# A decoder trunk on one core: the first product of every weight chunk in two halves of 128 columns

## The chip, the core and the metric

The kernel runs on one core of a Trainium2 chip. Its engines work at the same time, each on its own queue: TensorE (PE; its weight loads are listed as PEld), VectorE (DVE), ScalarE (ACT), GpSimd (POOL) and SyncE (SP), which issues most transfers here. The metric is the device time of one execution in microseconds.

## The reference

Two decoder layers over 256 tokens of width 2048, in float32. Cut to what matters:

```python
for l in range(DEPTH):                                   # DEPTH = 2
    u = rms_norm(h, norm1_g[l])
    (sc_x, sc_c, sc_b, m_cq, m_ckv, m_kr, g_q, g_k, g_v, g_z, g_a, g_b,
     r_q, r_f, r_i, r_z) = split_cols(u @ w_in[l])       # w_in: 2048 x 5840
    y_sc  = ...    # gated short convolution
    y_mla = ...    # latent attention: low-rank q, k, v by w_uq, w_ukv
    y_gdn = ...    # gated delta rule, chunks of 64
    y_hg  = ...    # HGRN2 recurrence, chunks of 64
    h = h + jnp.concatenate([y_sc, y_mla, y_gdn, y_hg], axis=-1) @ w_o[l]
    v_ff = rms_norm(h, norm2_g[l])
    h = h + jnp.square(jax.nn.relu(v_ff @ w_ff1[l])) @ w_ff2[l]   # 2048 -> 8192 -> 2048
return rms_norm(h, final_g)
```

## The kernel before

All weights pass once through the core as streams, one for each group of output columns: gk, krab, gz, gq, rz, gv, rf, rq, ri, cq, ckv, uqn, uqr, uk, uv, sx, sc, sb (the mixer), wo0 to wo3, and the MLP in four quarters q, each with four streams f1_q_0 to f1_q_3 (FF1) and four f2_q_0 to f2_q_3 (FF2). A stream has kt tiles of 128 rows (16 of them for a contraction over 2048) and m columns, mostly 512.

`stream` works through its weights in chunks. `_chunks` makes a chunk as many k-tiles as divide kt and fit 2048 columns: 4 k-tiles at m = 512 or 384, 8 at 256, all 16 at 72 (krab), and the whole stream for uqn (3 k-tiles, m = 512), uqr (3, 256) and uk (2, 512). `fetch` (L323) brings a chunk into one of three raw buffers over SP's queue. In pieces of up to 1024 columns ScalarE rounds it to fp32r, Ht (L354), and VectorE subtracts to get the rest, Lt (L355); there are four buffers of each. The activations (u, u2) are kept as such a pair too, `a[:, 0]` and `a[:, 1]`, 256 tokens wide. A product of the reference is then three matmuls: high x high, high x low, low x high.

In most streams the weights are the stationary operand and the 256 tokens pass through: for each column group j of 128 columns, for each k-tile of the chunk, L404, L405 and L406, adding up in one half of a PSUM bank. These are the 256-column streams. uv, wo and FF2 are token-major: the activations are stationary and 512 columns of weights pass (L368 to L370), in another branch of `stream`. The first product of a bank clears it (`start=`). For the six names in `HALVES` the very first product of the stream, and only that one, is issued as two matmuls of 128 tokens (L402) with the same weights:

```python
begin, end = opens and first and i == 0, closes and final and i == kc - 1
if begin and j == 0 and key in HALVES:
    for t in (slice(0, P), slice(P, T)):
        PE.matmul(o[:, t], lhsT=Hk[:, ms], rhs=a[:, 0, t], start=t.start == 0, stop=False)
else:
    PE.matmul(o, lhsT=Hk[:, ms], rhs=a[:, 0, :], start=begin, stop=False)
PE.matmul(o, lhsT=Hk[:, ms], rhs=a[:, 1, :], start=False, stop=False)
PE.matmul(o, lhsT=Lk[:, ms], rhs=a[:, 0, :], start=False, stop=end)
```

The mixer's own small matmuls (L711 to L1155; L971 is the HGRN2 levels, L873 and L877 the delta rule's steps) stand between the streams' products on TensorE. The order of each engine's instructions is set by a planner that plays the program through with estimated times; rounding, subtraction, transfers and evacuations have been given a high priority.

Of the kernel before, what the change touches and what calls it, by code (L numbers as in the profile page):

```python
# [33 lines left out]

COL = dict(sx=0, sc=512, sb=1024, cq=1536, ckv=1920, kr=2176, gq=2240, gk=2752, gv=3264, gz=3776,
           ab=4288, rq=4296, rf=4808, ri=5320, rz=5832)


HALVES = ("rz", "rf", "rq", "f1_1_0", "f1_2_0", "f1_3_0")

# [1 line left out]
def _chunks(kt, m):  # L44

    kc = max(c for c in range(1, kt + 1) if kt % c == 0 and c * m <= RAW_ELEMS)
    kp = min(kc, max(1, PIECE_ELEMS // m))
    if kp > 2:
        while kc % kp:
            kp -= 1  # L50
    return kc, kp
# [146 lines left out]
class Slots:  # L198
# [6 lines left out]
    def get(self, shape, dtype=F32):  # L205
        assert self.free, "no slot left"
        i = self.free.pop(0)
        self.low = min(self.low, len(self.free))
        self.k += 1
        t = self.pool.tile([shape[0], SLOT], dtype, tag=f"slot{i}", name=f"sl{self.k}", bufs=1)  # L210
        n = int(np.prod(shape[1:]))
        assert n <= SLOT
        v = t[:, :n]
        if len(shape) == 3:
            v = v.rearrange("p (a b) -> p a b", a=shape[1])
        elif len(shape) == 4:
            v = v.rearrange("p (a b c) -> p a b c", a=shape[1], b=shape[2])
        self.of[id(v)] = (i, v)
        return v
# [8 lines left out]
def trunk(ctx: ExitStack, tc: tile.TileContext, xT, x_d, fg_d, pos, wpk, par_d, cst_d, msk_d, out):  # L228
    nc = tc.nc
    V, S, G, PE = nc.vector, nc.scalar, nc.gpsimd, nc.tensor  # L230
# [75 lines left out]
    def main_bank(name):  # L306
        return psx.tile([P, 512], F32, tag="m", name=name, bufs=NMAIN)


    def fetch(l, key, c, between=None):  # L310
        off, kt, m = info[l, key]
        kc, _ = _chunks(kt, m)
        n = kc * m
        o = off + c * P * n
        raw = wp.tile([P, RAW_ELEMS], F32, tag="raw", name="raw", bufs=3)
        with tc.high_priority(AHEAD):
            src = wpk[l][o : o + P * n].rearrange("(p n) -> p n", p=P)

            for i in range(2 if between else 1):
                z = slice(i * n // 2, (i + 1) * n // 2) if between else slice(0, n)  # L320
                if between:
                    between(c * kc + i * kc // 2, c * kc + (i + 1) * kc // 2)
                nc.sync.dma_start(raw[:, z], src[:, z])  # L323
        return raw

    def stream(l, key, rhs, evac=None, order=None, token_major=None, banks=None, start=0, wide=False):

        off, kt, m = info[l, key]
        kc, kp = _chunks(kt, m)
        nm = (m + P - 1) // P
        if banks is not None:
            pss = banks
        elif token_major is None:
            pss = [main_bank(f"ps_{key}") for j in range(0, nm, 1 if wide else 2)]
        else:  # L340
            pss = [main_bank(f"ps_{key}") for j in range(2)]
        order = order or range(kt // kc)
        seen = start
        for c in order:
            early = l == 0 and key == "gk"
            raw = fetch(l, key, c, load_x if early else None)
            parts = []
            for k0 in range(0, kc, kp):
                ke = min(kp, kc - k0)
                src = raw[:, k0 * m : (k0 + ke) * m]  # L350
                Ht = wp.tile([P, PIECE_ELEMS], F32R, tag="H", name="Ht", bufs=4)
                Lt = wp.tile([P, PIECE_ELEMS], F32R, tag="L", name="Lt", bufs=4)
                with tc.high_priority(AHEAD):
                    S.copy(Ht[:, : ke * m], src)  # L354
                    V.tensor_tensor(Lt[:, : ke * m], src, Ht[:, : ke * m].bitcast(F32), ALU.subtract)  # L355
                H3 = Ht[:, : ke * m].rearrange("p (k m) -> p k m", k=ke)
                L3 = Lt[:, : ke * m].rearrange("p (k m) -> p k m", k=ke)
                parts += [(H3[:, k], L3[:, k], rhs(c * kc + k0 + k)) for k in range(ke)]
            first, final = seen == 0, seen + kc == kt
            seen += kc  # L360
            if early:
                first_split(c * kc, c * kc + kc)
            if token_major:
                for j in range(2):
                    ps, ms = pss[j], slice(j * P, j * P + P)
                    for i, (Hk, Lk, a) in enumerate(parts):
                        begin, end = first and i == 0, final and i == kc - 1
                        PE.matmul(ps, lhsT=a[:, 0, ms], rhs=Hk, start=begin, stop=False)  # L368
                        PE.matmul(ps, lhsT=a[:, 1, ms], rhs=Hk, start=False, stop=False)  # L369
                        PE.matmul(ps, lhsT=a[:, 0, ms], rhs=Lk, start=False, stop=end)  # L370
                    if final:
                        with tc.high_priority(AHEAD):
                            evac(j, ps)
                continue
            for j in range(nm if wide else 0):
                ps, ms = pss[j], slice(j * P, j * P + P)
                for i, (Hk, Lk, a) in enumerate(parts):
                    begin, end = first and i == 0, final and i == kc - 1

                    def high():  # L380
                        PE.matmul(ps, lhsT=Hk[:, ms], rhs=a.rearrange("p a t -> p (a t)"), start=begin, stop=end)

                    def low():
                        PE.matmul(ps[:, T:], lhsT=Lk[:, ms], rhs=a[:, 0, :], start=False, stop=False)

                    for f in (low, high) if end else (high, low):
                        f()
                if final:
                    with tc.high_priority(AHEAD):
                        evac(j, ps)  # L390
            for j in range(0 if wide else nm):
                ps = pss[j // 2]
                w = min(P, m - j * P)
                ms = slice(j * P, j * P + w)
                o = ps[:w, j % 2 * T : j % 2 * T + T]
                opens, closes = j % 2 == 0, j % 2 == 1 or j == nm - 1
                for i, (Hk, Lk, a) in enumerate(parts):
                    begin, end = opens and first and i == 0, closes and final and i == kc - 1
                    if begin and j == 0 and key in HALVES:

                        for t in (slice(0, P), slice(P, T)):
                            PE.matmul(o[:, t], lhsT=Hk[:, ms], rhs=a[:, 0, t], start=t.start == 0, stop=False)  # L402
                    else:
                        PE.matmul(o, lhsT=Hk[:, ms], rhs=a[:, 0, :], start=begin, stop=False)  # L404
                    PE.matmul(o, lhsT=Hk[:, ms], rhs=a[:, 1, :], start=False, stop=False)  # L405
                    PE.matmul(o, lhsT=Lk[:, ms], rhs=a[:, 0, :], start=False, stop=end)  # L406
                if final and closes:
                    n = j % 2 + 1
                    with tc.high_priority(AHEAD):
                        evac(j // 2, ps[:w, : n * T].rearrange("p (a t) -> p a t", a=n), n)  # L410
        return pss
# [120 lines left out]
    def first_split(k0, k1):  # L532

        with tc.high_priority(AHEAD):
            for k in range(k0, k1):
                scaled_split(u, k, xs[k // 4][:, k % 4], pc(0, "n1", k))
# [85 lines left out]
    for l in range(DEPTH):  # L622
# [41 lines left out]

        rawk = get((P, NH, T))
        stream(l, "gk", ua, to_slot(rawk))
        stream(l, "krab", ua, ev_krab)
        nc.scalar.dma_start(kr[64:, 0], kr[:64, 0])
        swap32(kr[:, 1], kr[:, 0])
# [3 lines left out]

        gz = get((P, NH, T))
        stream(l, "gz", ua, to_slot(gz))

        na = tmp.tile([8, 1], F32, tag="na", name="na", bufs=1)
# [8 lines left out]
        for tb in range(2):  # L686
            for i, src in enumerate((la, sg)):
                o = (tb * 2 + i) * 8
# [73 lines left out]
        rz = get((P, NH, T))  # L762
# [351 lines left out]
        for tb in range(2):  # L1114
# [5 lines left out]
            for g in range(NH // per):  # L1120
                ps = xps((P, per, n), "sc")
                for i in range(per):
# [3 lines left out]
                              start=False, stop=True)  # L1126
# [86 lines left out]
        for q in range(4):  # L1213
            a8 = [get((P, 2, 2, T), F32R) for _ in range(8)]
            a = lambda k, a8=a8: a8[k // 2][:, k % 2]
# [80 lines left out]
```

## Time and profile before

| | us |
|---|---|
| median of 3 runs | 2332.02 (2331.19 to 2332.23) |
| the profiled execution | 2331.44 |
| its span | 2329.7 |
| TensorE busy | 2296.3 |
| VectorE busy | 1416.7 |
| ScalarE busy | 1126.0 |
| GpSimd busy | 252.7 |

The span runs from the first to the last instruction of one profiled execution. An engine's busy time counts an instant once, however many of its instructions overlap there. Layer 0 lies at 0 to 1168 us (mixer up to 467, then the MLP), layer 1 behind it (mixer up to 1618).

### The profile page before, as it was taken

What the parts mean: (1) busy time and instruction counts of PE and PEld (TensorE: products, weight loads), DVE (VectorE), ACT (ScalarE), POOL (GpSimd) and SP (SyncE); (2) the same over time, 40 slices, a digit from 0 to 9 for tenths busy, and PEclk for the clock granted to TensorE, in tenths of its full rate; (3) what the DMA queues carried; (4) which work ended last, traced back from release to release, by engine and by line L of the source; (5) the groups of instructions that cost most, each with busy time, mean ns of one, the idle gap of its engine ahead of it and who ended that gap; (6) DMA issues with size and microseconds to landing.
All of it is one profiled execution on the core that took longest, in us unless ns stands there. A gap on an engine that the chain in (4) does not pass through costs nothing.

```text
span 2329.7 us, 38035 instructions
## 1 busy us (share of the span) xinstructions
PE 2296.3 (99%) x16060; PEld 2131.0 (91%) x16060; DVE 1416.7 (61%) x1585; ACT 1126.0 (48%) x1392; POOL 252.7 (11%) x175
## 2 busy tenths in 40 slices
PE   8999999999999999999999999999999999999997
PEld 8999999899899899899899998988988988988986
DVE  8888686555545545555578867865554554555454
ACT  6554555554344344344455647555443443443443
POOL 2322210000000000000013114000100100100100
PEclk9999999999999999999999999999999999999999
DMA  7453245555555555555545532555555555556553
GB/s 287 165 184 130 90 168 181 183 195 189 194 198 191 192 197 193 190 195 196 184 164 176 181 130 99 170 184 175 195 197 197 186 198 197 188 195 215 191 193 122
DMA packets 63754, 422.46 MB, mean 181 GB/s; under 512 B 7136, under 2 KB 10080, under 8 KB 15200
## 3 DMA queue, kind: packets, MB, share of 16 engines
q1 hardware_dynamic: 62656, 419.13, 51.7%
q8 instruction: 125, 2.05, 0.3%
q10 hardware_dynamic: 928, 0.92, 0.2%
q14 instruction: 45, 0.37, 0.0%
HBM read 417.00 MB, written 2.10 MB: 180 GB/s over the span
## 4 chain that ended last, share of the span: by engine, by line
PE 95%; DVE 3%; ACT 1%; issue 1%; DMA 0%; POOL 0%; SPq 0%; ACTq 0%; DVEq 0%
PE ps_f L405 10%; PE ps_f L406 10%; PE ps_f L370 10%; PE ps_f L369 10%; PE ps_f L368 10%; PE ps_f L404 10%; PE ps_wo L369 3%; PE ps_wo L368 2%; PE ps_wo L370 2%; PE lv L971 1%; DVE Lt L355 1%; PE ps_gq L404 1%; PE ps_gq L406 1%; PE ps_sb L404 1%; PE ps_gq L405 1%; PE ps_sb L406 1%
## 5 line engine op out<-in xcount | busy, mean ns | idle before, releaser
L355 DVE TENSOR_TENSOR Lt<-raw,Ht 128x1024 fp32r<-128x1024 f32 (+2 forms) x790 | 983.4, 1263 | 758.3 <-ACT Ht L354 736.3
L354 ACT CAST Ht<-raw 128x1024 fp32r<-128x1024 f32 (+2 forms) x790 | 804.5, 1043 | 852.9 <-PE ps_f L369 346.8
L405 PE MATMUL ps_f<-u,Ht 128*128 128x256 f32 x2048 | 565.9, 276 | 0.0
L406 PE MATMUL ps_f<-u,Lt 128*128 128x256 f32 x2048 | 565.5, 276 | 0.0
L404 PE MATMUL ps_f<-u,Ht 128*128 128x256 f32 x2042 | 563.7, 276 | 0.0
L370 PE MATMUL ps_f<-Lt,sl 128*128 128x512 f32 x1024 | 399.0, 390 | 0.0
L369 PE MATMUL ps_f<-Ht,sl 128*128 128x512 f32 x1024 | 398.5, 389 | 0.0
L368 PE MATMUL ps_f<-Ht,sl 128*128 128x512 f32 x1024 | 398.4, 389 | 0.0
L405 PEld LDWEIGHTS ps_f<-u,Ht 128*128 128x128 f32 x2048 | 384.5, 188 | 0.1
L406 PEld LDWEIGHTS ps_f<-u,Lt 128*128 128x128 f32 x2048 | 384.4, 188 | 0.0
L404 PEld LDWEIGHTS ps_f<-u,Ht 128*128 128x128 f32 x2042 | 383.3, 188 | 0.1
L369 PEld LDWEIGHTS ps_f<-Ht,sl 128*128 128x128 f32 x1024 | 192.2, 188 | 39.8
L370 PEld LDWEIGHTS ps_f<-Lt,sl 128*128 128x128 f32 x1024 | 192.2, 188 | 39.7
L368 PEld LDWEIGHTS ps_f<-Ht,sl 128*128 128x128 f32 x1024 | 192.2, 188 | 39.5
L1224 POOL TENSOR_TENSOR sl<-sl,sl 128x512 fp32r<-128x512 f32 x64 | 83.1, 1299 | 1316.1 <-ACT sl L1223 1105.3
L368 PE MATMUL ps_wo<-Ht,sl 128*128 128x512 f32 x256 | 100.5, 392 | 0.0
L370 PE MATMUL ps_wo<-Lt,sl 128*128 128x512 f32 x256 | 100.3, 393 | 0.0
L369 PE MATMUL ps_wo<-Ht,sl 128*128 128x512 f32 x256 | 99.8, 390 | 0.0
L1223 ACT CAST sl<-sl 128x512 fp32r<-128x512 f32 x64 | 39.8, 622 | 81.6 <-DVE sl L1222 81.6
L521 DVE SCALAR_TENSOR_TENSOR h<-ps_f,r2sq,h 128x512 f32<-128x512 f32 x64 | 47.9, 748 | 26.1 <-PE ps_f L370 26.1
L1221 ACT ACTIVATE sl<-ps_f 128x512 f32<-128x512 f32 x64 | 38.0, 593 | 49.4 <-PE ps_f L406 49.4
L1222 DVE TENSOR_TENSOR sl<-ps_f,sl 128x512 f32<-128x512 f32 x64 | 43.8, 685 | 23.4 <-ACT sl L1221 23.4
(404 smaller groups left out, 3636.5 us busy)
## 6 DMA issues: line engine op xcount, KB each, us to landing
raw<-w SPq DMA_DIRECT2D x376, 1024.0 KB, 4.8
raw<-w SPq DMA_DIRECT2D x10, 768.0 KB, 4.3
raw<-w SPq DMA_DIRECT2D x12, 512.0 KB, 7.5
sl<-xT SPq DMA_DIRECT2D x8, 256.0 KB, 7.8
h<-x SPq DMA_DIRECT2D x2, 1024.0 KB, 10.7
y<-h SPq DMA_DIRECT2D x8, 256.0 KB, 4.0
raw<-w SPq DMA_DIRECT2D x2, 576.0 KB, 7.2
sl<-fg SPq DMA_DIRECT2D x2, 512.0 KB, 4.7
```

Source lines behind the costliest of these rows:

```text
L354: S.copy(Ht[:, : ke * m], src)
L355: V.tensor_tensor(Lt[:, : ke * m], src, Ht[:, : ke * m].bitcast(F32), ALU.subtract)
L368: PE.matmul(ps, lhsT=a[:, 0, ms], rhs=Hk, start=begin, stop=False)
L369: PE.matmul(ps, lhsT=a[:, 1, ms], rhs=Hk, start=False, stop=False)
L370: PE.matmul(ps, lhsT=a[:, 0, ms], rhs=Lk, start=False, stop=end)
L404: PE.matmul(o, lhsT=Hk[:, ms], rhs=a[:, 0, :], start=begin, stop=False)
L405: PE.matmul(o, lhsT=Hk[:, ms], rhs=a[:, 1, :], start=False, stop=False)
L406: PE.matmul(o, lhsT=Lk[:, ms], rhs=a[:, 0, :], start=False, stop=end)
L521: V.scalar_tensor_tensor(z, ps, scale[:, tb : tb + 1], z, ALU.mult, ALU.add)
L1222: V.tensor_tensor(s_, ps, b_, ALU.mult)
L1223: S.copy(a2[:, :, 0, :], s_)
L1224: G.tensor_tensor(a2[:, :, 1, :], s_, a2[:, :, 0, :].bitcast(F32), ALU.subtract)
```

## The change

`HALVES` goes. Every chunk of a 256-column stream now issues its first product (column group 0, first k-tile) as two matmuls of 128 tokens each, with the same weights. Only where that product also opens the stream does its first half clear the bank; in later chunks both halves add to what is there.

```diff
-HALVES = ("rz", "rf", "rq", "f1_1_0", "f1_2_0", "f1_3_0")
...
                     begin, end = opens and first and i == 0, closes and final and i == kc - 1
-                    if begin and j == 0 and key in HALVES:
+                    if i == 0 and j == 0:
 
                         for t in (slice(0, P), slice(P, T)):
-                            PE.matmul(o[:, t], lhsT=Hk[:, ms], rhs=a[:, 0, t], start=t.start == 0, stop=False)
+                            PE.matmul(o[:, t], lhsT=Hk[:, ms], rhs=a[:, 0, t], start=begin and t.start == 0, stop=False)
                     else:
                         PE.matmul(o, lhsT=Hk[:, ms], rhs=a[:, 0, :], start=begin, stop=False)
```

## Rows read from the trace of the kernel before

**Rows 1.** The page: busy time by engine, and the last chain by engine.

```profile
PE 2296.3 (99%) x16060; PEld 2131.0 (91%) x16060; DVE 1416.7 (61%) x1585; ACT 1126.0 (48%) x1392; POOL 252.7 (11%) x175
...
PE 95%; DVE 3%; ACT 1%; issue 1%; DMA 0%; POOL 0%; SPq 0%; ACTq 0%; DVEq 0%
```

**Rows 2.** The page's groups: count, busy us and mean ns, idle before.

```profile
L404 PE MATMUL ps_f<-u,Ht 128*128 128x256 f32 x2042 | 563.7, 276 | 0.0
```

**Rows 3.** Busy time by stretch: length, engines in order, granted clock, DMA share, GB/s.

```profile
0.00:46.10 46.10, 38.40 (x272) 36.38 (x273) 37.44 (x57) 28.37 (x48) 11.75 (x17) 0.96 0.80 293
...
171.30:209.50 38.20, 36.82 (x323) 36.42 (x321) 35.79 (x57) 21.35 (x24) 10.84 (x3) 1.00 0.40 148
...
267.30:300.80 33.50, 28.46 (x200) 25.53 (x199) 24.32 (x29) 27.82 (x43) 14.70 (x8) 1.00 0.26 87
...
467.50:1168.20 700.70, 700.70 (x4644) 640.29 (x4644) 361.31 (x343) 311.86 (x354) 41.56 (x32) 1.00 0.55 193
...
1332.90:1342.40 9.50, 8.91 (x80) 8.71 (x78) 9.50 (x14) 6.86 (x9) 3.69 (x2) 1.00 0.31 110
...
1418.00:1451.40 33.40, 28.36 (x199) 25.46 (x198) 24.25 (x29) 27.72 (x42) 14.67 (x8) 1.00 0.25 86
```

**Rows 4.** Timeline where f1_1_0 opens: start us, us, engine, line, instruction.

```profile
642.68 0.33 PE L402 MATMUL ps_f<-u,Ht 128*128 128x128 f32 x2
642.79 0.19 PEld L405 LDWEIGHTS ps_f<-u,Ht 128*128 128x128 f32 x1
642.85 0.33 PE L405 MATMUL ps_f<-u,Ht 128*128 128x256 f32 x1
642.90 0.19 PEld L406 LDWEIGHTS ps_f<-u,Lt 128*128 128x128 f32 x1
643.02 0.28 PE L406 MATMUL ps_f<-u,Lt 128*128 128x256 f32 x1
643.02 0.19 PEld L404 LDWEIGHTS ps_f<-u,Ht 128*128 128x128 f32 x1
643.14 0.28 PE L404 MATMUL ps_f<-u,Ht 128*128 128x256 f32 x1
```

**Rows 5.** Line 402: duration ns min/median/max, first and last start us.

```profile
L402 PE MATMUL ps_f<-u,Ht x12: 222/248/273, 642.7 to 2141.8; 128*128 128x128 f32 x12
```

**Rows 6.** Timeline of TensorE at f1_1_0's second chunk, and where FF2 begins.

```profile
648.13 0.28 PE L406 MATMUL ps_f<-u,Lt 128*128 128x256 f32 x1
648.24 0.28 PE L404 MATMUL ps_f<-u,Ht 128*128 128x256 f32 x1
...
729.84 0.39 PE L368 MATMUL ps_f<-Ht,sl 128*128 128x512 f32 x1
```

**Rows 7.** Timeline of TensorE where rq opens.

```profile
166.31 0.33 PE L402 MATMUL ps_rq<-u,Ht 128*128 128x128 f32 x2
166.48 0.33 PE L405 MATMUL ps_rq<-u,Ht 128*128 128x256 f32 x1
166.65 0.28 PE L406 MATMUL ps_rq<-u,Lt 128*128 128x256 f32 x1
```

**Rows 8.** TensorE's waits: who waited for whom, total us, times, longest.

```profile
PE it L1065 <- ACT sl L1066: 3.6, 2, 1.8
PE ps_uv L370 <- DVE Lt L355: 3.3, 2, 1.7
PE ps_gk L406 <- DVE Lt L355: 2.6, 3, 1.6
PE ps_krab L406 <- DVE Lt L355: 1.9, 1, 1.9
PE ps_gk L404 <- ACT Ht L354: 1.3, 2, 0.8
...
PE ps_ri L406 <- DVE Lt L355: 0.6, 1, 0.6
```

**Rows 9.** TensorE alone by stretch, the same columns; the granted clock follows the count.

```profile
40.70:44.00 3.30, 3.30 (x18) 0.50 0.88 290
```

## The prediction

> **What bounds the kernel now.** I read the page's busy shares and its chain first: TensorE is busy for 2296.3 us of a span of 2329.7 us, and 95% of the chain that ended last is its own work [rows 1]. A matmul's busy time overlaps its neighbour's (a 256-column product is drawn 276 ns long [rows 2]), so that share alone does not say that TensorE is full; the starts in the timelines do [rows 4, 6]. In the second of the four quarters of layer 0's MLP the FF1 streams open at 642.68 us, with two halves that are there already, and the first FF2 product starts at 729.84 us [rows 4, 6]. Between them the code issues 4 streams x 16 k-tiles x 4 column groups x 3 = 768 products, one of them in two halves: 769 matmuls in 87.16 us, **0.1133 us each**, one slot. Sixteen chunks of weights begin in that time. I looked at one: the second chunk begins 4 x 4 x 3 + 1 = 49 slots after 642.68, at 648.24 us, and it starts 0.11 after the product ahead of it, like every other one [rows 6]. So there is no bubble at a chunk's beginning that two shorter products could fill. In that MLP VectorE is busy for 361 of 700.7 us and ScalarE for 312 [rows 3]; the chunks are ready in time.
>
> TensorE does wait in two places. At the start of layer 0 it is fed too slowly: 38.4 us busy of the first 46.1 [rows 3], with waits of 2.6, 1.9 and 1.3 us for Lt and Ht in gk and krab [rows 8]. In the middle of each layer, around the attention groups, it waits for the other engines: 1.38 us of 171.3 to 209.5, 5.04 of 267.3 to 300.8, and in layer 1 0.59 of 1332.9 to 1342.4 and 5.04 of 1418.0 to 1451.4 [rows 3]. That is 12.05 us in all.
>
> **The change, counted.** Until now only the very first product of six named streams was halved. Now the first k-tile of column group 0 of every chunk is. By the chunk rule (as many k-tiles as fit 2048 columns, dividing the k count) a layer's mixer has 11 streams of 512 columns with 4 chunks each (44), cq 4, ckv 2, krab 1, and uqn, uqr and uk 1 each: 54. FF1 has 16 streams of 4: 64. That is 118 a layer, 236 in all, 12 of them halved already, so **224 matmuls and 224 weight loads are added**, 122 in FF1 and 102 in the mixer. The wo, uv and FF2 streams take another branch. Nothing is removed, and no transfer, copy or subtraction is added. Both halves need what the whole product needed (the same Ht, the same tile of u), so nothing can start earlier.
>
> **Its price.** The trace holds the very operation, 24 halves of it. At 642.68 the pair starts; the next product (L405) starts at 642.85, the one behind it (L406) at 643.02, and from there on the starts are 0.11 to 0.12 apart again [rows 4]. From the first half to L406 it is 0.34 us, where two whole products take 2 x 0.1133 = 0.227. So a halved product costs 0.113 us more, a whole slot, although it streams the same 256 columns. The columns themselves do pass in half the time: the pair is drawn 0.33 us long and a half lasts up to 273 ns, so the second starts some 0.06 after the first [rows 4, 5]. But the weight loads behind the pair start at 642.79, 642.90 and 643.02, not closer than 0.11 [rows 4], and every matmul here brings its own. I read it so: loads have a pace of 0.11 us, like a 256-column product, and an extra load pushes all behind it by one slot. In rq, where 256-column products and not 512-column ones stand ahead of the pair, it is 166.31 to 166.65, 0.34 again [rows 7]. No row shows a pair at a chunk in mid-stream; rq's is the nearest, and I see no difference in kind. I take 0.1133. The starts are given to 0.01 us, and two readings agree, so I let it be 0.108 to 0.118.
>
> **What of it lies on the path.** The 122 in FF1 all do, since TensorE never pauses there: 122 x 0.1133 = 13.8 us. Of the 102 in the mixer:
> - The four of gk and the one of krab in layer 0 stand among waits for Lt and Ht of up to 1.9 us [rows 8], released by VectorE and ScalarE, which the pairs do not delay. These five cost nothing; with that cover gone, 0.6 us.
> - uqn, uqr and uk of both layers (six) come ahead of uv's two waits, 3.3 us together, for Lt, which VectorE writes [rows 8]: nothing, or 0.7 us uncovered.
> - VectorE is busy for 35.8 of the 38.2 us from 171.3 in layer 0 and for all 9.5 us from 1332.9 in layer 1, and there TensorE ends up waiting [rows 3] (0.6 us for ri's Lt in layer 1 [rows 8]). Eight chunks begin there (rq's second to fourth and ri's first three in layer 0, rq's fourth and ri's first in layer 1). But VectorE's own pieces wait for Ht, whose buffers TensorE gives back. So I let half of the eight be hidden, 4, with 0 and 8 as ends.
>
> That leaves 224 - 5 - 6 - 4 = 209 on the path, 209 x 0.1133 = **23.7 us**. Nothing else becomes late behind it: what follows a chunk's products (evacuations, the next pieces) moves with them, and the weight transfers gain 0.11 us per chunk.
>
> **Two side effects, bounded.** The clock: from 40.7 to 44.0 us the granted clock is 0.50, so 1.2 GHz [rows 9], after TensorE has stood for 1.9 us ahead of krab's first Lt [rows 8]. Eighteen matmuls pass in 3.3 us instead of 29: 11 x 0.1133 = 1.25 us lost. The pairs shorten the standstill by some 0.1 us only, so I let this stay as it is; it may go (-1.25) or come a second time (+1.25). The order: the small products of the mixer are placed between the streams by a planner that follows estimated times, and 224 more matmuls change its input. The two layers have different orders already, as the stalls show: 1.38 us against 0.59 in the stretches where ri begins [rows 3]. That is 0.8 us a layer, 1.6 in both, either way.
>
> **Sum.** The profiled execution took 2331.44 us (the span of 2329.7 and 1.7 around it), 0.58 under the runs' median of 2332.02. 2331.44 + 23.7 = 2355.1; on the median's scale 2355.7 us, 1.0% longer. Low end: 224 - 5 - 6 - 8 = 205 on the path at 0.108 are 22.1, less 1.25 and 1.6: 19.3, on the median 2351.3. High end: all 224 at 0.118 are 26.4, with 1.25, 1.6 and one more stall like the longest of the mixer (1.8 [rows 8]) 31.1: 2363.1.
>
> **Rivals.**
> 1. *The second load is hidden (not slower).* The place is the pair: the second half's load, the same weights again, runs beside the first half, and L405's beside the second. Then a pair takes twice the 0.06 between its halves, 0.12, and costs 0.007 us more than a whole product: 209 x 0.007 = 1.5 us, 2333.5 us, no change. It decides from the point at which L405 starts 0.12 behind the first half; the rows show 0.17, and another 0.17 to L406 [rows 4, 7]. Against it stands every pair of the trace. 3%. The Trainium skill's page "TensorE: Matmul & The Clock Gate", section "Back-to-back issue gap", would have it this way: it gives 134 cycles for 128 columns and 262 for 256, by which (an estimate from that page) a pair costs 2.5 ns and all 224 cost 0.6 us. The trace does not agree for this stream.
> 2. *Half hidden.* At a chunk in mid-stream only the 0.17 us to L405 is paid and L406 keeps its slot: a pair costs 0.057 us, 209 x 0.057 = 11.9, 2343.9 us. For it speaks only that the trace has no pair in mid-stream; against it, rq's. 4%.
> 3. *A worse order.* The planner puts small products where their inputs come too late, and the 12.05 us of mid-layer waits come once more: 2355.7 + 12.05 = 2367.8 us. For it: each of those waits hangs on the order; against it: the two orders that the trace has differ by 0.8 us a layer. 9%. The opposite, an order that closes them all, gives back half of the 23.7 us and is still slower, about 2343.7: 1%.
>
> **How the numbers follow.** The forecast has 83%, and its ends make the range, 2351 to 2363 us; the other cases, 17%, lie outside it. A measurement of this kernel can tell about 0.2%, 4.7 us, from no change. Slower: 83 + 4 + 9 + 1, less 1 for what I have not seen: 96%. Same: rival 1, 3%. Faster: 1%, since no wait on TensorE's path is one that a pair could end sooner.
>
> **What will show it.** The price is right if a pair at a chunk in mid-stream takes 0.34 us to L406, and the quarter that opened at 642.68 holds 769 + 15 = 784 matmuls in 784 x 0.1133 = 88.8 us instead of 87.16. It is wrong if that quarter stays near 87.2 us. The cover is right if the first 46 us, and the stretch from uqn to uv, keep their lengths. The order is right if from the first gz product to the first FF1 product a layer grows by 37 to 46 slots (46 pairs are new there), 4.2 to 5.2 us; more or less than that is the planner's, and the list of waits would name new pairs of lines. The forecast as a whole fails if matmuls with equal weights cost no second load, or if the order changes by more than the two layers now differ.

## The result and the profile after

| | before | after |
|---|---|---|
| median, us | 2332.12 (4 runs, 2331.19 to 2333.01) | 2355.06 (4 runs, 2354.18 to 2355.40) |
| profiled execution, us | 2331.44 | 2354.18 |
| its span, us | 2329.7 | 2352.3 |

The ratio is 1.0098 with a 95% interval of 1.0086 to 1.0110: slower by 1.0%. The forecast was 2355.7 us, the sum for the profiled execution 2355.1. The total is nearly exact, but, as the experiments show, several of its terms are not, and the prediction did not know what the pairs of the kernel before were doing.

The page of the changed kernel, busy time by engine and the last chain, beside [rows 1]:

```profile
PE 2319.7 (99%) x16284; PEld 2155.1 (92%) x16284; DVE 1419.9 (60%) x1585; ACT 1126.2 (48%) x1392; POOL 257.6 (11%) x175
...
PE 94%; DVE 2%; ACT 1%; issue 1%; POOL 0%; DMA 0%; SPq 0%; ACTq 0%; DVEq 0%; POOLq 0%
```

224 matmuls and 224 weight loads more, as counted. TensorE is busy for 23.4 us longer and the span is 22.6 us longer. The busy times of the other engines grow by 0.2 to 4.9 us in all. The extra matmuls lie on the path.

The timeline of TensorE in the same FF1 quarter as [rows 4, 6] (the lines of the code moved up by three: L399 is the pair, L401 to L403 the whole products, L365 FF2):

```profile
646.40 0.33 PE L399 MATMUL ps_f<-u,Ht 128*128 128x128 f32 x2
...
651.85 0.28 PE L403 MATMUL ps_f<-u,Lt 128*128 128x256 f32 x1
...
651.96 0.33 PE L399 MATMUL ps_f<-u,Ht 128*128 128x128 f32 x2
...
652.13 0.33 PE L402 MATMUL ps_f<-u,Ht 128*128 128x256 f32 x1
...
652.30 0.28 PE L403 MATMUL ps_f<-u,Lt 128*128 128x256 f32 x1
...
652.42 0.28 PE L401 MATMUL ps_f<-u,Ht 128*128 128x256 f32 x1
...
652.54 0.28 PE L402 MATMUL ps_f<-u,Ht 128*128 128x256 f32 x1
...
652.65 0.28 PE L403 MATMUL ps_f<-u,Lt 128*128 128x256 f32 x1
...
735.46 0.39 PE L365 MATMUL ps_f<-Ht,sl 128*128 128x512 f32 x1
```

A pair in mid-stream (at a later chunk of a stream, with 256-column products ahead of it) takes 0.34 us to the second product behind it, as at an opening. But the next starts are 0.12, 0.12 and 0.11 apart before the pace is back at 0.1133. The quarter lasts 735.46 - 646.40 = 89.06 us instead of 87.16: 1.90 us for 15 new pairs, **0.127 us each**, where the forecast had 0.1133 and 88.8 us. The first quarter of a layer, with 16 new pairs, grows by 1.98 us. FF1 in all: 2 x (1.98 + 3 x 1.90) = 15.4 us, forecast 13.8.

From the first gz to the first FF1 product, by stretch (length, busy time of PE, PEld, DVE, ACT and POOL with counts, granted clock, DMA share, GB/s); layer 0 and layer 1, first the kernel before, then the changed one:

```profile
46.13:467.54 421.41, 414.97 (x3139) 393.54 (x3138) 319.44 (x415) 230.11 (x307) 79.91 (x47) 1.00 0.46 161
1197.71:1618.17 420.46, 414.82 (x3139) 393.64 (x3138) 316.67 (x395) 233.50 (x313) 77.94 (x47) 1.00 0.47 161
```

```profile
44.53:469.28 424.75, 419.27 (x3185) 398.18 (x3184) 323.99 (x418) 230.67 (x308) 81.67 (x47) 1.00 0.45 160
1207.16:1633.00 425.84, 421.01 (x3185) 400.16 (x3184) 317.37 (x395) 234.17 (x313) 81.26 (x47) 0.99 0.46 159
```

With 46 new pairs each, layer 0 grows by 3.3 us and layer 1 by 5.4; the forecast was 4.2 to 5.2 for both. And gz of layer 0 begins 1.6 us earlier, at 44.53 instead of 46.13. Together these are -1.6 + 3.3 + 5.4 + 15.4 = 22.5 of the 22.6 us.

### The profile page after: what moved, and what is told of

The parts are those of the page before. It is cut to its first block, busy times and chain, and to the rows that moved or that the text cites. A ratio compares the mean times of both kernels' runs of the same rounds, so it can differ in the third digit from the quotient of the medians.

```text
span 2352.3 us, 38475 instructions
## 1 busy us (share of the span) xinstructions
PE 2319.7 (99%) x16284; PEld 2155.1 (92%) x16284; DVE 1419.9 (60%) x1585; ACT 1126.2 (48%) x1392; POOL 257.6 (11%) x175
## 4 chain that ended last, share of the span: by engine, by line
PE 94%; DVE 2%; ACT 1%; issue 1%; POOL 0%; DMA 0%; SPq 0%; ACTq 0%; DVEq 0%; POOLq 0%
PE ps_f L402 10%; PE ps_f L403 10%; PE ps_f L366 10%; PE ps_f L367 10%; PE ps_f L365 10%; PE ps_f L401 9%; PE ps_wo L367 2%; PE ps_wo L366 2%; PE ps_wo L365 2%; PE lv L968 1%; PE ps_f L399 1%; DVE Lt L352 1%; PE ps_gv L402 1%; PE ps_sb L402 1%; PE ps_sx L402 1%
## 5 line engine op out<-in xcount | busy, mean ns | idle before, releaser
L402 PE MATMUL ps_f<-u,Ht 128*128 128x256 f32 x2048 | 573.1, 280 | 0.0
L403 PE MATMUL ps_f<-u,Lt 128*128 128x256 f32 x2048 | 566.0, 276 | 0.0
L401 PE MATMUL ps_f<-u,Ht 128*128 128x256 f32 x1920 | 530.7, 276 | 0.0
L365 PE MATMUL ps_f<-Ht,sl 128*128 128x512 f32 x1024 | 398.4, 389 | 0.0
L403 PEld LDWEIGHTS ps_f<-u,Lt 128*128 128x128 f32 x2048 | 385.0, 188 | 0.0
L402 PEld LDWEIGHTS ps_f<-u,Ht 128*128 128x128 f32 x2048 | 384.9, 188 | 0.0
L401 PEld LDWEIGHTS ps_f<-u,Ht 128*128 128x128 f32 x1920 | 360.5, 188 | 0.0
L365 PEld LDWEIGHTS ps_f<-Ht,sl 128*128 128x128 f32 x1024 | 192.2, 188 | 39.8
L365 PE MATMUL ps_wo<-Ht,sl 128*128 128x512 f32 x256 | 100.5, 392 | 0.0
```

## Theories

**A**, the prediction's: a pair costs one slot of 0.1133 us on the path and does nothing else. **B**, formed when I laid the starts of all products in a row: 256-column products have *two* paces, 0.1133 and 0.118 us from start to start. Matmuls of another shape ahead of them can leave them at 0.118 (not all do, see below), they stay there, and a pair brings them back to 0.1133. The kernel before shows both on either side of rz's pair:

```profile
93.00 0.28 PE L406 MATMUL ps_gq<-u,Lt 128*128 128x256 f32 x1
...
93.36 0.28 PE L406 MATMUL ps_gq<-u,Lt 128*128 128x256 f32 x1
93.47 0.34 PE L402 MATMUL ps_rz<-u,Ht 128*128 128x128 f32 x2
...
94.29 0.28 PE L404 MATMUL ps_rz<-u,Ht 128*128 128x256 f32 x1
...
94.63 0.28 PE L404 MATMUL ps_rz<-u,Ht 128*128 128x256 f32 x1
```

Three gq products from 93.00 take 0.36 us, three rz products from 94.29 take 0.34. If B holds, a pair is not only a cost.

## Experiments: what a pair gives back

All edits are to the kernel before, in the condition of L399 (`H` stands for `begin and key in HALVES`). Where pairs stand at later chunks, `start=` is as in the change.

**No pair at all.**

```diff
-                    if begin and j == 0 and key in HALVES:
+                    if False:
```

> No product is halved (the 12 pairs of the kernel before go too). Theory A, of the prediction: a pair costs one slot of 0.1133 us wherever it stands and does nothing else, so 12 x 0.1133 = 1.4 us are saved: 2330.7 us. Theory B, formed from the changed kernel's trace: 256-column products have two paces, 0.1133 and 0.1178 us; behind matmuls of another shape (512-column, float32) they fall into the slower and stay in it, until something resets them, and a pair does. Then the six MLP quarters that open behind FF2 run their 768 FF1 products at 0.1178: 6 x (768 x 0.0045 - 0.11) = +20 us, and rf, rq with some +1: about 2353 us. Between them if the slow pace ends by itself at the next chunk (48 products x 0.0045 = 0.2 us each): 2332.

Measured: 2351.43 us against 2331.63, ratio 1.0085 (1.0070 to 1.0100). Twelve matmuls fewer, and 20 us slower. The second FF1 quarter, as a stretch of TensorE alone (length, busy, clock, DMA share, GB/s) and where it opens and ends:

```profile
643.64:734.09 90.45, 90.45 (x769) 1.00 0.53 185
...
643.64 0.28 PE L404 MATMUL ps_f<-u,Ht 128*128 128x256 f32 x1
...
734.09 0.39 PE L368 MATMUL ps_f<-Ht,sl 128*128 128x512 f32 x1
```

768 products in 90.45 us are 0.1178 each, at a granted clock of 1.00, through sixteen chunk beginnings without a pair and without a change of pace. Each of the six quarters that open behind FF2 is 3.3 us longer than in the kernel before: 19.8 us. Theory A falls, and so does the form in which a chunk's beginning ends the slow pace. That 19.8 is also the whole difference is partly chance. The openings of rz, rf and rq are slow too and add 0.72 us each, 4.4 in all. The order of the mixer's small matmuls changed as well: from ri to sx it takes 3.6 us less in layer 1 and 0.8 less in layer 0, and gz begins 0.5 us earlier.

The first quarter of each layer, which opens behind wo, is as long without pairs as before: 88.1 us in layer 0. It has a switch that is not a pair. In the kernel before, which has no pair there either:

```profile
468.84 0.38 PE L489 MATMUL tu<-cst,h 128*128 128x128 f32 x2
...
469.18 0.28 PE L404 MATMUL ps_f<-u,Ht 128*128 128x256 f32 x1
...
471.65 0.28 PE L404 MATMUL ps_f<-u,Ht 128*128 128x256 f32 x1
471.77 0.82 PE L489 MATMUL tu<-cst,h 128*128 128x128 f32 x6
...
472.67 0.28 PE L404 MATMUL ps_f<-u,Ht 128*128 128x256 f32 x1
...
477.77 0.28 PE L404 MATMUL ps_f<-u,Ht 128*128 128x256 f32 x1
```

Behind two of the float32 transposes of L489 the products stay slow: 21 starts in 2.47 us, 0.118 each. Behind six of them they are fast: 45 starts in 5.10 us, 0.1133 each. In the changed kernel two of them, at 470.54 us, even end the fast pace that the pair at 469.28 us had set. And gz, which opens behind krab's 72-column weights, is fast from its first product without any pair. Its 192 products take 0.1133 us each (the count takes in a neighbour at either end):

```profile
46.13:67.89 21.76, 21.76 (x194) 1.00 0.60 205
```

**The pair one stream later.**

```diff
-HALVES = ("rz", "rf", "rq", "f1_1_0", "f1_2_0", "f1_3_0")
+HALVES = ("rz", "rf", "rq", "f1_1_1", "f1_2_1", "f1_3_1")
```

> As the kernel before, but in the three quarters that open behind FF2 the pair stands at the opening of the second FF1 stream (f1_q_1) and not of the first. Theory B (the slow pace of 0.1178 stays until a pair, whatever the pair's place): the first stream's 192 products run at 0.1178, the other 576 at 0.1133, so 6 x 192 x 0.0045 = 5.2 us more, 2336.8 us; each of these quarters 88.0 us. Theory A, and the form of B in which only an opening right behind FF2 helps: 2331.6 (A) or the 20 us of the kernel without pairs, 2351 (opening only).

Measured: 2336.29 us against 2331.82, ratio 1.0020 (1.0010 to 1.0029). The opening, the pair, and the first FF2 product:

```profile
642.82 0.28 PE L404 MATMUL ps_f<-u,Ht 128*128 128x256 f32 x1
...
665.43 0.33 PE L402 MATMUL ps_f<-u,Ht 128*128 128x128 f32 x2
...
730.83 0.39 PE L368 MATMUL ps_f<-Ht,sl 128*128 128x512 f32 x1
```

The 192 products up to the pair take 22.61 us, 0.1178 each; the 577 from the pair on take 65.40, 0.1133 each. The pair switches the pace here too, 192 products into the slow stretch, and the quarter is 0.85 us longer, as B says. Six such quarters make 5.1 us; the medians differ by 4.5.

**Two whole products in place of the two halves, at the six openings.**

```diff
-                    if begin and j == 0 and key in HALVES:
+                    if False:
...
+                    elif begin and j == 0 and key in HALVES:
+                        for again in range(2):
+                            PE.matmul(o, lhsT=Hk[:, ms], rhs=a[:, 0, :], start=begin and not again, stop=False)
```

> As the kernel before, but the six openings issue the whole first product twice and not in two halves (it is counted twice in the output). As many matmuls and loads as before. Theory B with the short product as the cause of the reset: a second whole product does not reset, the quarters run 769 at 0.1178, 90.6 us instead of 87.16: about 20 us more, 2352. Rival B2, in which any additional load or the mere repeat of the weights resets: 87.2 us a quarter, 2332.

Measured: 2357.78 us against 2331.82, ratio 1.0110 (1.0095 to 1.0125). The opening, the product behind it, and the first FF2 product (the lines are three further down):

```profile
644.61 0.40 PE L405 MATMUL ps_f<-u,Ht 128*128 128x256 f32 x2
644.85 0.28 PE L408 MATMUL ps_f<-u,Ht 128*128 128x256 f32 x1
...
735.18 0.40 PE L368 MATMUL ps_f<-Ht,sl 128*128 128x512 f32 x1
```

769 matmuls in 90.57 us: slow throughout. So in a pair it is not the additional load, nor the repeated weights, but the short products that switch the pace. My number was too low, since I had counted FF1 alone: the three mixer openings of each layer now run 193 matmuls at 0.118 as well, 0.84 us each. 6 x 3.41 + 6 x 0.84 = 25.5 us, of 26.0 measured; the waits of the mixer shifted by parts of a us besides.

## Experiments: what a pair costs

**Pairs in FF1 alone, and in the mixer alone.**

```diff
-                    if begin and j == 0 and key in HALVES:
+                    if i == 0 and j == 0 and (key[:2] == "f1" or H):      # ff1
+                    if i == 0 and j == 0 and (key[:2] != "f1" or H):      # mixer
```

> Pairs at every chunk of FF1, and in the mixer only the three openings of the kernel before. Theory A: 122 x 0.1133 = 13.8 us, 2345.9. Theory B: in a run that is already at the fast pace a pair in mid-stream costs what the changed kernel's quarters show, 1.90 us per 15, 0.127 each: 122 x 0.127 = 15.5, 2347.6, and the mixers stay as before.

> Pairs at every chunk of the mixer's streams, and in FF1 only the three openings of the kernel before. Theory A: 87 on the path x 0.1133 = 9.9 us, 2342.0. Theory B: the pairs give part back by resetting the slow pace (about 1600 products of the kernel before run at 0.118, 7 us in all): +2 to +7 us, 2334 to 2339. Where in that range hangs on the clock: with a half clock in the middle of layer 1, as the changed kernel has, 2339; without it 2336.

Measured: FF1 alone 2347.95 us against 2331.63, ratio 1.0071 (1.0054 to 1.0088), its span 15.6 us longer; the mixer alone 2339.90 (2338.54 to 2345.26), ratio 1.0039 (1.0024 to 1.0054), its span 6.8 us longer. The spans add up to 22.4 of the 22.6 us of the whole change. In FF1 the price is B's 0.127. The mixer's 102 pairs cost 6.8 us in the profile, 0.067 each, about half of it; a start that is 1.8 us shorter by its clock and 1.7 us of other waits in layer 1 (both below) are in that and nearly cancel. By the medians the mixer's part is 8.3 us: its four runs spread over 6.7 us, and the profiled one was the fastest.

**The whole first product twice, at the 122 other chunks of FF1.**

```diff
+                    elif i == 0 and j == 0 and key[:2] == "f1":
+                        for again in range(2):
+                            PE.matmul(o, lhsT=Hk[:, ms], rhs=a[:, 0, :], start=begin and not again, stop=False)
```

> As with pairs at every chunk of FF1, but instead of two halves the whole first product of the chunk is issued twice (122 of them; that product is counted twice in the output). The same number of matmuls and of weight loads, twice the columns. If loads set the price of a pair (A and B), a second whole product costs no more than a pair: 0.1133 to 0.127 each, 2345.9 to 2347.6. B in its narrower form, that the 0.013 beyond a slot come from the short products and not from the load, expects 0.1133: 2345.9 flat. If columns set it, a second whole product costs 0.1133 and a pair should have cost nothing.

Measured: 2346.26 us against 2331.63, ratio 1.0061 (1.0046 to 1.0076). A chunk's beginning in the second quarter:

```profile
650.64 0.39 PE L405 MATMUL ps_f<-u,Ht 128*128 128x256 f32 x2
650.87 0.28 PE L408 MATMUL ps_f<-u,Ht 128*128 128x256 f32 x1
```

The quarter grows by 1.70 us for 15, 0.1133 each. A second whole product with 256 columns more costs *less* than cutting the first one in two. The 0.013 us that a pair costs beyond a slot belongs to the short products.

**Four parts of 64 columns, at the same 122 chunks.**

```diff
+                    elif i == 0 and j == 0 and key[:2] == "f1":
+                        for t in [slice(x, x + 64) for x in range(0, T, 64)]:
+                            PE.matmul(o[:, t], lhsT=Hk[:, ms], rhs=a[:, 0, t], start=begin and t.start == 0, stop=False)
```

> Pairs only at the six openings of the kernel before; at the other 122 chunks of FF1 the first product is issued in four parts of 64 columns. If loads set the price (one load per 0.11 us), each costs three slots more than a whole product, 3 x 0.1133 = 0.34, with the 0.013 behind it 0.35 or more: 122 x 0.35 = 43 us, 2374 to 2376. If the price were one for being split at all (0.127), 2347.

Measured: 2374.68 us against 2331.82, ratio 1.0183 (1.0166 to 1.0200). One such place:

```profile
654.66 0.53 PE L405 MATMUL ps_f<-u,Ht 128*128 128x64 f32 x4
655.02 0.37 PE L408 MATMUL ps_f<-u,Ht 128*128 128x256 f32 x1
655.23 0.28 PE L409 MATMUL ps_f<-u,Lt 128*128 128x256 f32 x1
```

The quarter grows by 5.40 us for 15, 0.36 each, for three loads more and the same columns: 0.12 per load. So the price follows the loads, not the columns. No matmul here goes without a load of its own, so a load and whatever else one more matmul brings are not told apart. The Trainium skill's page "TensorE: Matmul & The Clock Gate", section "LDWEIGHTS (loading the stationary operand)", gives a load as its columns over 1.2 GHz, 107 ns for 128 by an estimate from it; the 0.12 measured is that and a tenth more. The gaps of the same page of the Trainium skill, section "Back-to-back issue gap", that the prediction set beside its first rival do not hold here. That section gives them for an isolated matmul, and says that in a stream of loads and matmuls both set the spacing.

**The pair at the third k-tile of the chunk.**

```diff
-                    if begin and j == 0 and key in HALVES:
+                    if j == 0 and ((i == 2 and key[:2] == "f1") or H):
```

> Pairs at the six openings of the kernel before, and at every chunk of FF1 in column group 0 at the third k-tile (i == 2), not the first: 128 pairs added. If a chunk's beginning is a place like any other (A and B), each costs 0.127 as at the first k-tile: 128 x 0.127 = 16.2 us, 2348.1. If the price at the first k-tile holds something of the chunk's beginning, a wait for its first Ht, it is nearer to one slot: 128 x 0.113 = 14.5, 2346.3.

Measured: 2347.42 us against 2332.57, ratio 1.0064 (1.0050 to 1.0077). In the profile a quarter grows by 2.03 us for 16 pairs, 0.127 each (1.99 in the first quarter of a layer). That is 2 x (1.99 + 3 x 2.03) = 16.2 us; the medians differ by 14.9, and in the profile the difference lies in the first 46 us, which are 1.2 us shorter (of that below). The beginning of a chunk is a place like any other, as the prediction had it.

## Experiments: the start, and pairs where they should pay

**Pairs in gk and krab of layer 0 alone.**

```diff
-                    if begin and j == 0 and key in HALVES:
+                    if j == 0 and (H or (i == 0 and l == 0 and key in ("gk", "krab"))):
```

> As the kernel before, with pairs also at the four chunks of gk and the one of krab in layer 0 alone. Prediction's cover: these five cost nothing, since TensorE waits there for Lt and Ht. If the pairs are also what keeps TensorE's clock from falling to 0.50 at 41 to 44 us, the first gz product comes 1.6 to 1.9 us earlier, 2329.9; if that fall is a matter of the single execution and not of the pairs, 2331.6 and no clear difference. Should they cost their five slots, 2332.2.

Measured: 2331.61 us (10 runs, 2329.85 to 2332.25) against 2331.82 (19 runs, 2329.90 to 2332.89), ratio 0.9999 (0.9990 to 1.0008). In its profile TensorE from 40.7 to 44.0 us, beside [rows 9]:

```profile
40.70:44.00 3.30, 3.30 (x30) 1.00 0.83 281
```

Here the clock did not fall, 30 matmuls pass in place of 18, and gz begins 1.5 us earlier. But the runs are no faster than those of the kernel before, and the kernel with the pair at the third k-tile, which has no pair in gk or krab, did not show the fall either. In the profiles that lack the fall and where gz begins earlier, it does so by 1.2 to 1.8 us. The profiled execution of this kernel was the fastest of its ten, at a mean granted clock of 0.997; others went down to 0.995, and those of the kernel before have 0.994 to 0.997. So time at the lower clock comes or stays away from one execution to the next. That the pairs have no part in it is not shown: all three profiled kernels with pairs in gk and krab (this one, the changed kernel, the mixer alone) lack the fall at 41 to 44 us, and of the nine others two do. The five pairs in gk and krab cost nothing that can be measured, as predicted.

**Pairs only where a long slow stretch follows.**

```diff
-                    if begin and j == 0 and key in HALVES:
+                    if i == 0 and j == 0 and ((begin and key in HALVES[3:] + ("rf",))
+                                              or (c == 2 and (key == "gq" or key == "gk" and l == 1))):
```

> Pairs only where a long run at 0.1178 follows: the openings of rf, f1_1_0, f1_2_0 and f1_3_0 as before, the third chunk of gq in both layers and of gk in layer 1; rz and rq lose theirs, since they then open in a fast run. Theory B: three pairs give back 96 x 0.0045 - 0.127 = 0.3 us each, four pairs fewer save 0.113 to 0.127 each: 1.4 us less, 2330.4, ratio 0.9994, provided that the order stays. Theory A (pairs only cost): one pair fewer, 0.1 us less, no difference.

Measured: 2329.88 us (11 runs) against 2332.57 (15 runs), ratio 0.9990 (0.9981 to 0.9999). This is the fastest version, by 0.1%, but the gain is not the one foreseen. Around gq's third chunk:

```profile
82.07 0.22 PE L402 MATMUL ps_gq<-u,Ht 128*128 128x128 f32 x1
82.13 0.68 PE L468 MATMUL l<-sl,ones_r 128*128 128x512 f32 x2
82.65 0.22 PE L402 MATMUL ps_gq<-u,Ht 128*128 128x128 f32 x1
82.71 0.33 PE L405 MATMUL ps_gq<-u,Ht 128*128 128x256 f32 x1
...
93.95 0.28 PE L404 MATMUL ps_rz<-u,Ht 128*128 128x256 f32 x1
...
94.54 0.28 PE L406 MATMUL ps_rz<-u,Lt 128*128 128x256 f32 x1
```

The planner put two 512-column matmuls between the halves. That pair switches nothing: rz opens slow (five products in 0.59 us, 0.118 each) and, without a pair of its own, takes 0.72 us more in each layer. Where the pair stayed whole, B's numbers came out: gk in layer 1 takes 23.57 us instead of 23.86, and rq without its pair behind rf, which ends at the fast pace, 0.13 us less. The largest gain, some 3 us, is a different order in the middle of layer 1: from ri to sx it takes 108.5 us, and 111.6 in the kernel before. That order came with this version and was not sought; the kernel without pairs has the same order there (108.0 us). Why the planner chose it stays open. The profiled execution is 0.7 us shorter than that of before, the median 2.7.

## Why the prediction was right, and where it was not

- **The count and the path** were right: 224 matmuls, no cover in FF1, and the weight transfers and other engines indifferent. The cover ahead of uv held where the order stayed: from uqn to sx layer 0 took 15.5 us before and after. The first rival (the second load hidden), the second (half hidden) and the third (12 us of new waits) did not come about.
- **The price was mis-sized**: 0.1133 us by the openings [rows 4, 7], 0.127 in mid-stream. Taking the openings as "no difference in kind" failed in size: behind a mid-stream pair the next three starts come 0.003 to 0.006 us late each. This term was 1.6 us too small in FF1. That the price goes by loads and not by columns was borne out (four parts: 0.12 per load).
- **What a pair gives** was missed altogether. The prediction called the chunk's beginning free of bubbles, which is true, and concluded that a pair can end nothing. But it had looked at a quarter whose pace a pair had already set. In the mixer, where slow stretches are frequent, a pair gives part of its price back: in layer 0 TensorE is busy for 4.3 us longer with 46 new pairs, 0.093 each and not 0.127, and it waits 1.0 us less (6.44 and 5.48 us of the two stretches shown). So this layer grew by 3.3 and not by 4.2 to 5.2 us. In FF1 nearly all pairs met stretches that were fast already and gave nothing.
- **The clock**: the fall at 41 to 44 us was taken to stay; in the profile of after it is gone (-1.6 us at gz with the covered pairs). The time at the lower clock varies from one execution to the next; whether the pairs in gk and krab make this fall rarer is not settled.
- **The order** did change in layer 1, by more than 0.8 us. TensorE's longest waits there after 1300 us, first before, then after (total us, times, longest); last, after, TensorE alone from 1444.9 us:

```profile
PE it L1065 <- ACT sl L1066: 1.8, 1, 1.8
PE ps_uv L370 <- DVE Lt L355: 1.7, 1, 1.7
...
PE ps_uqn L404 <- ACT sl L449: 0.6, 1, 0.6
```

```profile
PE ho L854 <- ACT sl L1063: 2.1, 1, 2.1
PE it L1062 <- ACT sl L1063: 1.5, 1, 1.5
PE lr L1038 <- POOL sl L1036: 1.1, 1, 1.1
```

```profile
1444.90:1451.50 6.60, 4.97 (x17) 0.53 0.01 2
```

Three waits in a row within 8 us, and then a granted clock of 0.53, mostly the lower level of 1.2 GHz, for 6.6 us. From the first ckv product of layer 1 to uqn's it takes 38.9 us instead of 35.0, 3.9 more, and uv's wait, which is gone, gives 2.2 back: 1.7 us net. The mixer-only kernel has the same waits (2.0, 1.5 and 1.1 us), the FF1-only kernel has not, so it goes with the mixer's pairs, by way of the order.

So the terms were FF1 +1.6, the clock -1.6, and the two mixers some -1 us from the forecast: the total came out right partly by luck, because these cancel.

## What to carry to other kernels

A saturated TensorE can still have two paces, as here. Read them from the starts of a long stretch, not from the busy share, and compare stretches that open behind different shapes. A split product cost about a weight load here, not columns, so put one only at the head of a long stretch that would otherwise go at the slower pace, and see to it that nothing is scheduled between its halves. Where a planner orders the work, a count of slots is good to a few microseconds only, since an edit can move the order.

## What the runs showed that was not expected

256-column products of 32-bit weights run at 0.1133 or at 0.1178 us each at the same granted clock, and a stretch of them with nothing in between keeps its pace as far as it was followed here, 768 products. FF2's 384 products of 512 columns ahead lead into the slower one. Two products of 128 columns with nothing between them switch to the faster one within five products, and so do six float32 transposes of L489 in the first FF1 quarter. Two such transposes do not, nor do two whole products with the same weights, chunk beginnings, or two halves with 512-column products between them. Which matmuls of other shapes lead into which pace was not sorted out: gz behind krab is fast without a pair. What in the engine keeps the pace, and what the short product changes, no run here settles.
